# Decay rows by a DRAM round trip: eight broadcast loads in place of 24 matmuls in a chunked scan

## The chip, the cores and the metric

The kernel runs on one core of a Trainium2 chip. The metric is the device time of one execution in microseconds (us); three runs of the kernel before were timed, and one execution of it was profiled.

## The reference, cut to what matters

The layer has a mixer (a state-space scan with 8 heads in 2 groups beside 8 attention heads), an output projection with a norm, and a mixture of 16 experts with a second norm, on 512 tokens of 1024 channels. The change touches one matrix of the scan. With `da = dt * a` per token and head, cumulated within a chunk, the reference has

```
a_cum = jnp.cumsum(da, axis=2)
seg = a_cum[:, :, :, None] - a_cum[:, :, None, :]
lmat = jnp.exp(jnp.where(tri, seg, -jnp.inf))
cb = jnp.einsum('bclgn,bcsgn->bclsg', cc, bc)
y_diag = jnp.einsum('bclsg,bclsgr,bcsgrp->bclgrp', cb, lmat, xdt)
```

So for each chunk and head a matrix exp(a_cum[l] - a_cum[s]) is needed for s <= l, and zero above; it is multiplied by C B^T. The kernel takes chunks of 128 tokens (4 of them) where the reference takes 64; the result is the same sum.

## The kernel before, in words

One core does everything in two phases. The first has the input projection, the scan, the attention and the output projection (until about 303 us of the span), with the router after it; the second has the experts, whose weights stream in from DRAM. All tiles of 4 KB a partition come from one pool of 31 slabs (`U`, L163), handed out in the order of the program text, each as an earlier one is released.

TensorE (PE) runs in the order of the program text. Work is written as generators that yield TensorE microseconds, and `weave` (L866) lets the fill stream (projections of group 1, values, queries and keys) run for as long as the chain asks. For VectorE (DVE), ScalarE (ACT), GpSimd (POOL) and SyncE's DMA queue (SP) no order is written down here: the framework's planner places their instructions by its own model of the time, and each engine then runs its queue in that order. The DMA queue of SP waits in place: an issue that waits for its buffer holds those behind it. Its loads around the scan are the projection weights `wr` (L224), 512 KB each, three buffers.

`gates` (L355) makes the decays. `pcum` (L396) are sums of `da` over the tokens of a chunk by a matmul with a triangle of ones (`triones`, L316); `acum` (L398) is [token, (chunk, head)] with the totals beside it. L414 transposes it to 64 rows (chunk, head), ACT and DVE split these into two exact parts `acT` (L416), and POOL spreads them over a group's four heads with a mask, `RL` (L420, four instructions of 64x512). The masks come from POOL instructions at the start (`hmask` L317 to L320, `cself` L322 to L326) and a cast by DVE (`csel` L327).

`scan` (L532) runs once a group, `decay` (L542) once a chunk and group, eight times in all. TensorE puts row l of the cumulated decays on all partitions with two matmuls 128x512 (L547: `csel` picks the chunk's rows of `RL`) and adds the causal mask with a third (L548), all into the PSUM bank `pl`. Three more make C B^T in `pcb` (L551). Then DVE subtracts the column of `acum` (L553, one instruction 128x512, from PSUM), ACT takes the exponential (L555), DVE multiplies by `pcb` (L556), and ACT and DVE split the product into `mt` (L557, through L103 and L104). `mt` is read by the matmuls of `py` (L586, L588). The decays of chunks 0 and 1 stand ahead of the loop (L567, L569), the one of chunk c+2 in the middle of chunk c (L602).

Beside these, `conv2` (L434) runs four DVE instructions for each block of 128 channels: three taps (L437), a correction of three columns (L438), and the gate (L440) behind ACT's tanh (L439). `conv_in` (L428) empties the PSUM bank of a projection (L429, ACT). POOL splits weights: `wl` (L234, 128x512, four a unit).

Of the kernel before, what the change touches and what calls it, by code (L numbers as in the profile page):

```python
# [7 lines left out]
F32 = mybir.dt.float32  # L8
F32R = mybir.dt.float32r
# [7 lines left out]
P = 128  # L17
S = 512
D = 1024
NT = S // P  # L20
# [52 lines left out]
# whose down projections follow an expert's gate and up projections  # L73
DOWN = [[]] + [[e - 1] for e in range(1, NEXP - 3)] + [[NEXP - 4, NEXP - 3], [NEXP - 2], [NEXP - 1]]
# order of the steps of the last norms: of a tile's, or the last expert's
# [7 lines left out]
def hybrid_layer(ctx: ExitStack, tc: tile.TileContext, x, xT, wu, w16, bT, bz, bv, b16, cw, cb,  # L83
# [22 lines left out]
    # ---- constants that depend on shapes alone  # L106
# [10 lines left out]
    # strict[j, l] = 1 where j < l  # L117
# [10 lines left out]
    # -big above the diagonal (column > row), and below it  # L128
# [11 lines left out]
    def rsqrt(o, var, mult, add, eng=V):  # L140
        """o = (var * mult + add) ** -0.5 on [P, n]"""
        eng.tensor_scalar(o, var, mult, add, op0=OP.mult, op1=OP.add)
        G.tensor_tensor(o, o, mhalf[:, : o.shape[1]], op=OP.pow)
# [5 lines left out]
    # tokens' places with each expert (1 and up, 0 for none), and what an expert's list holds  # L149
    # of a token: its number (less BIG) in two parts and its weight in three, exact in bfloat16  # L150
# [8 lines left out]
    # slabs of 4 KB and of 1 KB a partition, shared by all phases  # L159
# [17 lines left out]
    # ---- x^T and the columns of w_in as exact pairs of float32r parts  # L177
# [7 lines left out]
    def first_x(q, n):  # L185
        """x^T of two blocks of channels, in n parts: first the loads, then the splits"""
# [14 lines left out]
    def first_w(u, q, n):  # L201
        """half of a unit's columns, likewise"""
# [38 lines left out]
    # The tensor engine runs in the order of emission. Work is written as generators that  # L241
    # yield the tensor engine's microseconds, so that independent streams can be woven.
    def proj_T(u, m, r):
        """r gets out[channel, token] of 128 channels of a unit"""
        pt = bank("pj", "pjT")
        i = 0
        for k in range(KC):
            h_, l_ = units[u][k // 4]
            for w_, x_ in ((h_, xh), (h_, xl), (l_, xh)):
                T.matmul(pt, lhsT=w_[:, k % 4, m * P:(m + 1) * P], rhs=x_[k], start=(i == 0), stop=(i == 23))  # L250
                i += 1
            yield 0.64
        r.append(pt)

    def proj_T2(u, r):
        """both halves of a unit together, block by block as these arrive"""
# [10 lines left out]
    def proj_R(u, t, r):  # L267
        """r gets out[token, 256 channels] for one tile of tokens"""
# [10 lines left out]
    # ---- the first loads, in the order of their use  # L279
# [9 lines left out]
    # ---- per-channel parameters  # L289
# [17 lines left out]
    # rows (chunk, head) of a 64-row table: which head, which chunk  # L307
    hmask = const.tile([64, 8], F32, name="hmask")
    triones, csel = halves("csel")
    csel = csel[:64].rearrange("p (c l) -> p c l", l=P)  # L310
    # triones[j, l] = 1 where j <= l
    trionesf, cself = halves("cself", F32)
# [4 lines left out]
    G.memset(hmask, 0.0)  # L317
    for c in range(NT):
        G.affine_select(out=hmask, in_=hmask, compare_op=OP.not_equal, fill=1.0, base=-8 * c,
                        pattern=[[-1, 8]], channel_multiplier=1)  # L320
    cself = cself[:64].rearrange("p (c l) -> p c l", l=P)
    G.memset(cself, 1.0)  # L322
    G.affine_select(out=cself, in_=cself, compare_op=OP.is_ge, fill=0.0, base=0,
                    pattern=[[-8, NT], [0, P]], channel_multiplier=1)
    G.affine_select(out=cself, in_=cself, compare_op=OP.is_ge, fill=0.0, base=7,
                    pattern=[[8, NT], [0, P]], channel_multiplier=-1)  # L326
    V.tensor_copy(csel, cself)  # L327
    # bias of the convolution's input: what all four taps add, and what the first
    # three tokens lack of it
# [16 lines left out]
    # ---- dt and the forget gates: [token, tile, (dt 8 | f 8)]  # L346
# [6 lines left out]
    RL = {}  # L353

    def gates():  # L355
# [15 lines left out]
        # softplus(v) = max(v, 0) + log1p(exp(-|v|)); log1p(e) = 2 atanh(e / (2 + e))  # L371
# [13 lines left out]
        # decays: da = dt * a, a = -exp(a_log)  # L385
        V.scalar_tensor_tensor(da, sp[:, :, 0:8], -1.0, an[:, None, :].to_broadcast([P, NT, 8]), op0=OP.mult, op1=OP.mult)
        V.tensor_scalar(dth, sp[:, :, 0:8], 0.5, None, op0=OP.mult)
        # 8 log f of head h on 16 copies each
# [5 lines left out]
        # cumulative sums within 128-token chunks, and their totals  # L394
# [8 lines left out]
        # rows -8 F[s]: partition (a, h) holds head h  # L403
# [8 lines left out]
        # the chunks' cumulative sums as rows (chunk, head), spread over a group's heads  # L412
        pa = bank("t", "pa")
        T.transpose(pa[:64, :P], acum, identf)  # L414
        ath, atl = (t_[:64] for t_ in halves("acT"))
        split(ath[:, :P], atl[:, :P], pa[:64, :P])  # L416
        for g in range(2):
            RL[g] = halves(f"RL{g}")
            for o_, a_ in zip(RL[g], (ath, atl)):
                G.tensor_tensor(o_[:64].rearrange("p (h l) -> p h l", l=P),  # L420
                                a_[:, None, :P].bitcast(F32).to_broadcast([64, 4, P]),
                                hmask[:, 4 * g:4 * g + 4, None].to_broadcast([64, 4, P]), op=OP.mult)
# [3 lines left out]
    # ---- state-space heads, one group of four heads at a time  # L426
# [6 lines left out]
    def conv2(in_, blk):  # L433
        """2 silu(conv(proj + bias)) of 128 channels: [channel, token]"""  # L434
# [12 lines left out]
    def tt4(o, a, sc4, op, eng=V):  # L447
        """o[p, 256] = a[p, 256] op sc4[p, head]"""
# [8 lines left out]
    def prep(g):  # L457
        """projections, convolution and operands of a group's scan"""
# [37 lines left out]
        # hi and lo parts side by side, so that one pass serves both  # L496
# [35 lines left out]
    def scan(g):  # L532
        """yields the time that the tensor engine may be given to other work"""
# [8 lines left out]
        def decay(c):  # L542
            # decay matrix times C B^T: [s, (head, l)]
            cs = slice(c * P, (c + 1) * P)
            pl = bank("s", "pl")
            for i in range(2):
                T.matmul(pl, lhsT=csel[:, c], rhs=RL[g][i][:64], start=(i == 0), stop=False)  # L547
            T.matmul(pl, lhsT=identb, rhs=maskl[:, None, :].to_broadcast([P, 4, P]), start=False, stop=True)  # L548
            pcb = bank("t", "pcb")[:, :P]
            for i, (b_, c_) in enumerate((("bh", "ch"), ("bh", "cl"), ("bl", "ch"))):  # L550
                T.matmul(pcb, lhsT=w[b_][:, cs], rhs=w[c_][:, cs], start=(i == 0), stop=(i == 2))  # L551
            lt = U("lt")[:, :512].rearrange("p (h l) -> p h l", l=P)
            V.tensor_tensor(lt, pl.rearrange("p (h l) -> p h l", l=P),  # L553
                            ac3[:, c, hs][:, :, None].to_broadcast([P, 4, P]), op=OP.subtract)
# [16 lines left out]
        for c in range(NT):  # L571
# [37 lines left out]
            # 2 silu(z) y, normed over the group's channels  # L609
# [18 lines left out]
    # ---- attention  # L628
    # (a head's hi and lo parts of v lie side by side, and those of its q one over the other,
    # so that one pass serves both)  # L630
# [56 lines left out]
    def head_S(hd, t):  # L687
# [9 lines left out]
        # -logits, and minus their maximum  # L697
# [42 lines left out]
    def heads():  # L740
        """yields the time that the tensor engine may be given to other work"""
# [42 lines left out]
    # ---- output projection; the state-space half of it fills the end of the attention  # L784
# [32 lines left out]
    # ---- router on rows u before their norm: logits = rs (u g wr - mu 1 g wr) + (b wr + br)  # L817
# [19 lines left out]
    # ---- weaving  # L837
# [54 lines left out]
    # ---- expert weights stream in from here on  # L892
    raw = {}

    def pieces():
        """the experts' weights in the order of their use: (expert, piece)"""
# [32 lines left out]
    # ---- experts  # L929
# [605 lines left out]
```

## Time and profile before

| what | us |
|---|---|
| median of three runs | 652.01 |
| lowest, highest | 650.62, 652.3 |
| span of the profiled execution (first to last instruction) | 649.7 |
| TensorE busy in the span | 586.1 |
| VectorE busy | 529.2 |
| ScalarE busy | 415.5 |
| GpSimd busy | 248.7 |

The own time of the profiled execution is not among the three runs that are given: its span stands 2.3 us under their median, and that difference is taken as what lies around the span. In the profile every row has a start or a count, a busy time, the engine, the line (L553 is line 553) and the tiles (out<-in). What stands behind an arrow in brackets is the idle time before the row and what ended it. A busy TensorE is back to back, not at its peak.

### The profile page before, as it was taken

The page shows a single profiled execution, that of the slowest core. Times are in us where ns is not written, and L with a number is a line of the kernel's source. Part 1 is how long each engine was busy: PE and PEld are TensorE (multiplying, and loading weights), DVE is VectorE, ACT ScalarE, POOL GpSimd, SP SyncE. Part 2 cuts the span into 40 slices and gives each one's busy share as a digit, 9 for nine tenths or more (in the row PEclk, how much of TensorE's full clock was granted, in tenths as well). Part 3 has the DMA queues.
Part 4 walks back from the last instruction along what each step waited for, and adds up shares of the span by engine and source line. Part 5 has one row for each costly group of instructions (what it writes and reads, how often), then busy time and mean ns, then how long its engine had stood idle before and what let it go on. Part 6 is the DMA issues. An engine that isn't in the chain of part 4 may idle for free.

```text
span 649.7 us, 9097 instructions
## 1 busy us (share of the span) xinstructions
PE 586.1 (90%) x3007; PEld 477.0 (73%) x3007; DVE 529.2 (81%) x869; ACT 415.5 (64%) x629; POOL 248.7 (38%) x248
## 2 busy tenths in 40 slices
PE   5888996999999999999398999999999999999950
PEld 4677786888776767788277888888888888877830
DVE  3986789688658797765879999999999999999673
ACT  5443353443577875523267888888888888887770
POOL 6537623733452341015614223333333322310282
PEclk9897997999999999998589999999999999999985
DMA  8421122211111174994888999999999999992342
GB/s 263 137 74 54 65 66 66 82 66 64 66 66 45 47 238 134 369 370 165 307 293 307 320 371 358 382 361 352 346 350 341 366 343 361 322 361 55 115 176 83
DMA packets 61702, 141.39 MB, mean 218 GB/s; under 512 B 9987, under 2 KB 10003, under 8 KB 61648
## 3 DMA queue, kind: packets, MB, share of 16 engines
q1 hardware_dynamic: 55168, 125.79, 54.1%
q0 software_dynamic: 5904, 12.85, 7.1%
q10 hardware_dynamic: 576, 2.10, 0.8%
q8 instruction: 25, 0.41, 0.3%
q14 instruction: 29, 0.24, 0.1%
HBM read 134.69 MB, written 14.68 MB: 230 GB/s over the span
## 4 chain that ended last, share of the span: by engine, by line
PE 62%; DVE 13%; ACT 6%; issue 6%; DMA 6%; POOL 5%; SPq 0%; POOLq 0%; ACTq 0%; DVEq 0%
PE pw L809 6%; PE pg L1003 5%; PE pg L1005 4%; PE pg L1004 4%; PE py L1037 4%; PE pu L1003 4%; PE pu L1005 4%; PE pu L1004 4%; PE py L1039 4%; PE py L1038 4%; PE pjT L250 4%; PE pjR L274 3%; DVE acc L437 3%; PE pxg L979 2%; DMA wr<-in_wu 1%
## 5 line engine op out<-in xcount | busy, mean ns | idle before, releaser
L986 ACT ACTIVATE eh<-wf 128x1024 fp32r<-128x1024 f32 x192 | 203.1, 1061 | 49.8 <-PE pg L1005 15.2
L234 POOL TENSOR_TENSOR wl<-wr,wh 128x512 fp32r<-128x512 f32 x40 | 57.0, 1449 | 45.0 <-ACT wh L229 42.2
L957 POOL DMA_INDIRECT xg<-hb,ix x16 | 21.1, 1317 | 112.7 <-PE pg L1005 107.5
L1043 POOL DMA_INDIRECT ub<-yo,ix x15 | 27.2, 1811 | 88.7 <-ACT at L103 54.4
L1037 PE MATMUL py<-eh,at 128*128 128x512 f32 x128 | 52.5, 410 | 2.7 <-ACT at L103 2.5
L1003 PE MATMUL pg<-eh,xgh 128*128 128x512 f32 x128 | 53.1, 415 | 0.8 <-ACT xgh L103 0.8
L1039 PE MATMUL py<-eh,at 128*128 128x512 f32 x128 | 50.9, 398 | 0.0
L1005 PE MATMUL pg<-eh,xgl 128*128 128x512 f32 x128 | 50.7, 396 | 0.0
L1003 PE MATMUL pu<-eh,xgh 128*128 128x512 f32 x128 | 50.0, 391 | 0.0
L1005 PE MATMUL pu<-eh,xgl 128*128 128x512 f32 x128 | 49.9, 390 | 0.0
L250 PE MATMUL pjT<-xh,wh 128*128 128x512 f32 x112 | 46.3, 413 | 1.6 <-DVE kl L672 1.6
L274 PE MATMUL pjR<-wh,xh 128*128 128x256 f32 x128 | 39.3, 307 | 8.6 <-ACT acc L429 7.6
L250 PE MATMUL pjT<-xh,wl 128*128 128x512 f32 x112 | 44.1, 394 | 0.0
L250 PE MATMUL pjT<-xl,wh 128*128 128x512 f32 x112 | 43.9, 392 | 0.0
L936 POOL TENSOR_SCALAR se<-seats,place 128x128 bf16<-128x128 f32 x56 | 43.5, 792 | 0.5
L274 PE MATMUL pjR<-wl,xh 128*128 128x256 f32 x128 | 38.1, 298 | 0.0
L274 PE MATMUL pjR<-wh,xl 128*128 128x256 f32 x128 | 38.0, 297 | 0.0
L274 PEld LDWEIGHTS pjR<-wh,xh 128*128 128x128 f32 x128 | 26.3, 206 | 9.3 <-ACT acc L429 8.0
L1037 PEld LDWEIGHTS py<-eh,at 128*128 128x128 f32 x128 | 24.5, 191 | 8.6 <-ACT at L103 2.7
L1005 PEld LDWEIGHTS pg<-eh,xgl 128*128 128x128 f32 x128 | 24.3, 190 | 6.1 <-DVE xgl L104 0.8
L1039 PEld LDWEIGHTS py<-eh,at 128*128 128x128 f32 x128 | 24.4, 191 | 5.9 <-DVE at L104 0.8
L1003 PEld LDWEIGHTS pg<-eh,xgh 128*128 128x128 f32 x128 | 24.3, 190 | 5.0 <-ACT xgh L103 1.2
(951 smaller groups left out, 1757.7 us busy)
## 6 DMA issues: line engine op xcount, KB each, us to landing
wf<-in_w_up SPq DMA_DIRECT2D x64, 512.0 KB
wf<-in_w_gate SPq DMA_DIRECT2D x64, 512.0 KB
wf<-in_w_down SPq DMA_DIRECT2D x60, 512.0 KB
wr<-in_wu SPq DMA_DIRECT2D x22, 512.0 KB
wor<-in_w_out SPq DMA_DIRECT2D x8, 512.0 KB
hh<-in_x SPq DMA_DIRECT2D x4, 512.0 KB
wf<-in_w_down POOLq DMA_DIRECT2D x4, 512.0 KB, 7.9
u<-ub SPq DMA_DIRECT2D x4, 512.0 KB
```

The costliest lines, as they stand in the source:

```text
L234: G.tensor_tensor(l_[:, j], wr_[:, j], h_[:, j].bitcast(F32), op=OP.subtract)
L250: T.matmul(pt, lhsT=w_[:, k % 4, m * P:(m + 1) * P], rhs=x_[k], start=(i == 0), stop=(i == 23))
L274: T.matmul(pt, lhsT=x_[k][:, t * P:(t + 1) * P], rhs=w_[:, k % 4, :], start=(i == 0), stop=(i == 23))
L809: T.matmul(pw, lhsT=m_[k][:, ts_], rhs=wo[k][w_][:, c_], start=(i == 0), stop=(i == 11))
L936: eng.tensor_scalar(r[t], seats, place_(t), None, op0=OP.is_equal)
L986: A.activation(h_, src, AF.Copy)
L1003: T.matmul(pt, lhsT=h_[:, k], rhs=wh_[:, f], start=(k == 0), stop=False)
L1004: T.matmul(pt, lhsT=h_[:, k], rhs=wl_[:, f], start=False, stop=False)
L1005: T.matmul(pt, lhsT=l_[:, k], rhs=wh_[:, f], start=False, stop=(k == KC - 1))
L1037: T.matmul(pt, lhsT=h_[:, f], rhs=wh_[:, c_], start=(f == 0), stop=False)
L1039: T.matmul(pt, lhsT=l_[:, f], rhs=wh_[:, c_], start=False, stop=(f == 3))
L1043: G.indirect_dma_start(out=ub, out_offset=bass.IndirectOffsetOnAxis(ap=ix, axis=0), in_=yo, in_offset=None, bounds_check=S - 1, oob_is_err ...
```

## The change

`gates` no longer makes `RL`: it transposes the 32 rows of cumulated decays, copies them to SBUF with ACT and writes them to a DRAM tile `ad` [chunk, head, token] through SP's queue. `decay` loads the four rows of its group and chunk onto all 128 partitions (`al`, 2 KB a partition) through SP's queue, and DVE subtracts the column and adds the mask, one instruction a head, in place of the single subtraction. The three matmuls of `pl` are gone, and `hmask`, `csel` and their making. The rest of the diff deletes comments.

```diff
-    hmask = const.tile([64, 8], F32, name="hmask")
-    triones, csel = halves("csel")
-    csel = csel[:64].rearrange("p (c l) -> p c l", l=P)
-    trionesf, cself = halves("cself", F32)
+    triones, trionesf = U("triones", F32R)[:, :512], U("trionesf")[:, :512]
     G.memset(trionesf, 1.0)
     G.affine_select(out=trionesf, in_=trionesf, compare_op=OP.is_ge, fill=0.0, base=0,
                     pattern=[[1, S]], channel_multiplier=-1)
     V.tensor_copy(triones, trionesf)
-    G.memset(hmask, 0.0)
-    for c in range(NT):
-        G.affine_select(out=hmask, in_=hmask, compare_op=OP.not_equal, fill=1.0, base=-8 * c,
-                        pattern=[[-1, 8]], channel_multiplier=1)
-    cself = cself[:64].rearrange("p (c l) -> p c l", l=P)
-    G.memset(cself, 1.0)
-    G.affine_select(out=cself, in_=cself, compare_op=OP.is_ge, fill=0.0, base=0,
-                    pattern=[[-8, NT], [0, P]], channel_multiplier=1)
-    G.affine_select(out=cself, in_=cself, compare_op=OP.is_ge, fill=0.0, base=7,
-                    pattern=[[8, NT], [0, P]], channel_multiplier=-1)
-    V.tensor_copy(csel, cself)
...
-    RL = {}
+    ad = tc.dram_tile([NT, 8, P], F32, name="ad")
...
         pa = bank("t", "pa")
-        T.transpose(pa[:64, :P], acum, identf)
-        ath, atl = (t_[:64] for t_ in halves("acT"))
-        split(ath[:, :P], atl[:, :P], pa[:64, :P])
-        for g in range(2):
-            RL[g] = halves(f"RL{g}")
-            for o_, a_ in zip(RL[g], (ath, atl)):
-                G.tensor_tensor(o_[:64].rearrange("p (h l) -> p h l", l=P),
-                                a_[:, None, :P].bitcast(F32).to_broadcast([64, 4, P]),
-                                hmask[:, 4 * g:4 * g + 4, None].to_broadcast([64, 4, P]), op=OP.mult)
+        T.transpose(pa[:32, :P], acum[:, 0:32], identf)
+        at_ = U("acT")[:32, :P]
+        A.activation(at_, pa[:32, :P], AF.Copy)
+        SY.dma_start(ad.rearrange("c h l -> (c h) l"), at_)
...
         def decay(c):
             cs = slice(c * P, (c + 1) * P)
-            pl = bank("s", "pl")
-            for i in range(2):
-                T.matmul(pl, lhsT=csel[:, c], rhs=RL[g][i][:64], start=(i == 0), stop=False)
-            T.matmul(pl, lhsT=identb, rhs=maskl[:, None, :].to_broadcast([P, 4, P]), start=False, stop=True)
+            al = U("al")[:, :512].rearrange("p (h l) -> p h l", l=P)
+            SY.dma_start(al, ad[c:c + 1, hs, :].to_broadcast([P, 4, P]))
...
             lt = U("lt")[:, :512].rearrange("p (h l) -> p h l", l=P)
-            V.tensor_tensor(lt, pl.rearrange("p (h l) -> p h l", l=P),
-                            ac3[:, c, hs][:, :, None].to_broadcast([P, 4, P]), op=OP.subtract)
+            for r in range(4):
+                V.scalar_tensor_tensor(lt[:, r], al[:, r], ac3[:, c, 4 * g + r:4 * g + r + 1], maskl, op0=OP.subtract, op1=OP.add)
             A.activation(lt, lt, AF.Exp)
```

## Rows read from the trace of the kernel before

**Rows 1.** Stages: length, busy PE, PEld, DVE, ACT, POOL (count), clock, DMA, GB/s.

```profile
48.00:64.00 16.00, 12.40 (x79) 12.03 (x80) 10.95 (x19) 6.14 (x14) 12.01 (x13) 0.79 0.20 66
64.00:80.00 16.00, 16.00 (x78) 12.01 (x77) 11.50 (x19) 7.25 (x13) 9.96 (x10) 1.00 0.20 66
80.00:96.00 16.00, 15.61 (x85) 12.77 (x84) 14.19 (x28) 8.20 (x16) 4.36 (x5) 1.00 0.20 67
96.00:112.00 16.00, 10.89 (x62) 10.47 (x61) 14.99 (x27) 7.85 (x15) 6.91 (x6) 0.79 0.21 67
...
128.00:144.00 16.00, 15.69 (x123) 14.43 (x121) 12.66 (x27) 8.15 (x19) 6.27 (x5) 1.00 0.24 81
144.00:160.00 16.00, 15.25 (x104) 13.88 (x105) 14.02 (x32) 6.22 (x16) 5.87 (x5) 1.00 0.11 34
...
400.00:432.00 32.00, 32.00 (x158) 26.28 (x157) 30.64 (x39) 26.74 (x32) 10.99 (x12) 1.00 1.00 358
```

**Rows 2.** The chain that ended last, 56 to 65 us: start, length, work.

```profile
56.41 4.36 PE pjR L274 x24
...
60.98 2.86 PE pjR L274 x24
...
64.28 0.66 PE pl L547 x2
64.94 0.32 PE pl L548
```

**Rows 3.** Timeline of VectorE at the start: start, busy, line, out<-in.

```profile
17.49 1.65 DVE L231 TENSOR_TENSOR wl<-wr,wh 128x1024 fp32r<-128x1024 f32 x1
19.06 0.41 DVE L327 CAST csel<-cself 64x512 fp32r<-64x512 f32 x1
19.39 1.21 DVE L231 TENSOR_TENSOR wl<-wr,wh 128x1024 fp32r<-128x1024 f32 x1
```

**Rows 4.** Timelines of GpSimd and of VectorE, 49 to 56 us.

```profile
49.84 5.63 POOL L420 TENSOR_TENSOR RL<-acT,hmask 64x512 fp32r<-64x512 f32 x4
...
49.66 2.22 DVE L437 SCALAR_TENSOR_TENSOR acc<-acc,cw_sb 128x511 f32<-128x511 f32 x2
...
52.13 1.19 DVE L437 SCALAR_TENSOR_TENSOR acc<-acc,cw_sb 128x509 f32<-128x509 f32 x1
53.24 0.99 DVE L438 TENSOR_TENSOR acc<-acc,lack 128x3 f32<-128x3 f32 x1
...
54.99 1.03 DVE L440 SCALAR_TENSOR_TENSOR acc<-acc 128x512 f32<-128x512 f32 x1 [0.42 <-ACT acc L439]
```

**Rows 5.** The same instructions of VectorE while GpSimd stands idle, 90 to 92 us.

```profile
90.93 0.74 DVE L437 SCALAR_TENSOR_TENSOR acc<-acc,cw_sb 128x509 f32<-128x509 f32 x1
91.59 0.16 DVE L438 TENSOR_TENSOR acc<-acc,lack 128x3 f32<-128x3 f32 x1
```

**Rows 6.** VectorE's subtractions for `lt` and `v`, by tile: min/median/max ns, starts.

```profile
L553 DVE TENSOR_TENSOR lt<-pl,acum x8: 675/684/692, 67.2 to 149.8; 128x512 f32<-128x512 f32 x8
...
L104 DVE TENSOR_TENSOR v<-vf,v x16: 281/284/1378, 128.5 to 156.8; 128x128 fp32r<-128x128 f32 x16
```

**Rows 7.** Groups of VectorE, 40 to 176 us, shapes apart: busy us, mean ns.

```profile
L104 DVE TENSOR_TENSOR v<-vf,v 128x128 fp32r<-128x128 f32 x16 | 7.2, 489 | 0.4 <-ACT v L103 0.4
```

**Rows 8.** A decay's subtraction, and the idle time of GpSimd around it.

```profile
93.45 0.68 DVE L553 TENSOR_TENSOR lt<-pl,acum 128x512 f32<-128x512 f32 x1
...
95.94 0.67 POOL L143 TENSOR_TENSOR rst<-rst,mhalf 128x1 f32<-128x1 f32 x1 [8.49 <-DVE rst L142]
```

**Rows 9.** ACT's copy of the rows, SP's next issue behind it, and one 256 KB broadcast load.

```profile
48.66 0.26 ACT L103 ACTIVATE acT<-pa 64x128 fp32r<-64x128 f32 x1
...
66.35 0.33 SPq L224 DMA_DIRECT2D wr<-in_wu  x1
...
L635 SPq DMA_DIRECT2D bv_sb<-in_bv x1: 376/376/376, 123.0 to 123.0; - x1
...
L646 DVE TENSOR_TENSOR vf<-pjR,bv_sb x8: 411/418/425, 127.3 to 154.0; 128x256 f32<-128x256 f32 x8
```

## The prediction

> **What bounds the kernel now.** The page's first part comes first: TensorE is busy for most of the span, VectorE next. An average over stages says nothing of one place, so the table of stages follows, then the chain that ended last, and the timelines of VectorE, GpSimd and SP. In the table of stages [rows 1] the reader is to see two regimes. TensorE is full at 64 to 80 us (16.00 of 16), and nearly so at 80 to 96, 128 to 144 and 144 to 160. Between, at 96 to 112, it has 10.89 of 16 while VectorE has 14.99: there VectorE is the bound, and TensorE waits for it. VectorE has little room at 80 to 96 (14.19) and at 144 to 160 (14.02) either. From 400 us on TensorE is full (32.00 of 32), so time won before is kept, one for one, unless the weights' loads fall behind; those start when the first phase gives its slabs free, so they move with it.
>
> In the chain [rows 2] the decays' matmuls stand on the path: 0.66 us for the two of L547 and 0.32 for the mask of L548, 0.98 us a decay, behind pjR matmuls of the fill stream. The chain's stretch before them goes over VectorE's conv instructions at 49 to 56 us, and these are long there only because GpSimd makes `RL` at the same time: three taps and the correction take 2.22, 1.19 and 0.99 us [rows 4], where at 90 us, with GpSimd idle, the same forms take 0.74 and 0.16 [rows 5].
>
> **The start.** GpSimd makes fewer masks and VectorE loses the cast of `csel`, 0.41 us. The subtraction of `wl` beside the masks took 1.65 us, the next one 1.21 [rows 3]. If the first also gets 1.21, VectorE is 0.44 + 0.41 = 0.85 us earlier where the convolution starts. I take -0.85; the bound on the other side is 0, if a load is late next.
>
> **RL goes.** Four GpSimd instructions, 5.63 us [rows 4]. A free pair of taps costs one step and one duration, 91.59 - 90.93 = 0.66, and 0.74, together 1.40 us [rows 5]. So the pair gives back 2.22 - 1.40 = 0.82, the third tap 1.19 - 0.74 = 0.45, the correction 0.99 - 0.16 = 0.83: 2.10 us, all ahead of the gate of L440, for which TensorE's next transposes wait. Between 0 and 2.10 I take 2.10, since nothing else of GpSimd's stands in those 6 us. The gate is left at its 1.03 us. The split of `acT` on VectorE goes too; it hid in a wait for ACT and counts nothing.
>
> **TensorE's clock.** At 48 to 64 us the granted clock was 0.79 [rows 1], behind idle TensorE, and 24 pjR matmuls took 4.36 us, the next 24 2.86 [rows 2]. With 2.10 us less idle ahead the first may come nearer to the second: between 0 and 1.50 us. I take 0.5, nearer to none, because part of that idle time stays.
>
> **The eight decays' matmuls.** 8 x 0.98 = 7.84 us of TensorE go. Where TensorE is full they count: those of chunks 0 and 1 of group 0, at 64 to 80 us, give 1.96 us. Chunks 2 and 3 come just ahead of the stretch where TensorE waits for VectorE; I count nothing for them (bound 1.96). Of group 1, whose last subtraction starts at 149.8 [rows 6], in nearly full stages [rows 1], I count three of four, 2.94 us (bounds 1.96 and 3.92).
>
> **VectorE's four instructions for one.** The subtraction takes 684 ns at the median [rows 6]. No 128x128 instruction with a pointer scalar is in the trace; the nearest is the 128x128 subtraction of `v` from SBUF, 284 ns at the median [rows 6]. Behind one another such instructions step by 0.08 us less than they last (0.74 against 0.66 [rows 5]), so four make 0.284 + 3 x 0.204 = 0.90 us, 0.22 more a decay, 1.8 in all. On the path I count the three decays where VectorE is short: +0.6 (bounds 0 and 1.8). [...]
>
> **GpSimd and VectorE together.** L553 reads PSUM and one SBUF tile and never stretched: 675 to 692 ns over eight [rows 6]. The new instructions read `al` and the mask, both in SBUF, like the taps, which did stretch. Lower bound: nothing, since seven of the eight subtractions stood where GpSimd was idle, as at 93.45 within an idle time of 8.49 us [rows 8]. Upper: the 16 subtractions of `v` of 128x128 took 489 ns on average against 281 at the least [rows 6, 7], 0.21 more, times 32 is 6.7 us. I take one decay's worth on the path, 4 x 0.21 = +0.8, nearer to the idle places.
>
> **The new loads.** ACT's copy, now one in place of a split, ends at 48.92; the write of 16 KB and then a broadcast load follow on SP's queue. The nearest row is a 256 KB broadcast load issued at 123.0 whose first reader ran at 127.3 [rows 9], so at most 4.3 us. Two in a row end before 48.9 + 8.6 = 57.5, and the first use was at 67.2. SP issues nothing before 66.35 [rows 9]; its wait for the write holds nobody. The other loads need a slab, and with `RL` and the masks gone three long-held slabs are free. DMA share is 0.20 there [rows 1]; 2 MB more are no load. I cost all this at nothing. ACT gains nothing; its exponential is the same.
>
> **Sum.** -0.85 - 2.10 - 0.5 - 1.96 - 2.94 + 0.6 + 0.8 = -6.95 us. The profiled span is 649.7, so 642.75; the median stands 2.3 us above that span, which gives 645.0 us. That is 1.1% faster. Its own range, with the bounds above mixed, is about 641 to 649.
>
> **Rivals.** *VectorE hides it.* Where TensorE waits for VectorE in any case, TensorE's savings turn into longer waits: the 4.9 us of matmuls and the 0.5 of clock fall away, and -0.85 - 2.10 + 0.6 + 0.8 = -1.55 remains: 650.5. For it: VectorE's 14.99 and 14.02 of 16. Against it: 16.00 of 16 for TensorE at 64 to 80. Chance 0.17.
>
> *Slower: the two engines lock each other.* If the mask additions fall into GpSimd's bursts of weight splits, each waits for a GpSimd instruction, as the correction of L438 did for 0.83 us: 4 x 0.83 = 3.3 us a decay. Five decays stand where VectorE is short (two of group 0, three of group 1): 16.6 us, less the 8.35 saved, plus 0.6, is +8.9, or 660.9; with four of them hit 657.5. It decides from 7.75 us on the path, between two and three decays. Against it speaks that seven of eight places are free now; for it that the planner may move them. [...] Chance 0.12.
>
> *The rows come late.* If the planner puts the first load behind the blocked weight load, it is issued at 66.7 and lands at 71.0, 3.8 us behind the old subtraction. Then what was saved before it is lost in a wait of TensorE, and +3.8 - 0.98 - 2.94 + 1.4 = +1.3 gives 653.3. It would mean also that the change does not do what it says, since a DMA's wait then stands in place of the matmuls. Chance 0.07.
>
> **Numbers.** A measurement of this kernel tells about 0.3%, 2 us, from no change. Forecast 0.64, hidden 0.17, locked 0.12, late 0.07. The range 640.5 to 653.5 goes from the forecast with more of the clock and of the matmuls up to the late rows, and leaves out most of the locked case and the forecast's far ends, about 0.18. Faster: the forecast and a third of the hidden case, 0.70. Same: the rest of the hidden case and most of the late one, 0.17. Slower: 0.13.
>
> **What would show it.** Right: no matmul of `pl`; the taps at 49 us at 0.74; mask additions of about 0.28 us each; every `al` landed well before its first reader; TensorE's transposes near 56 us some 3 us earlier, and the attention 7 us earlier. Wrong: mask additions of 0.5 us and more on average, an idle VectorE that a load ends, or a TensorE whose idle time at 96 to 112 us grows by what the matmuls gave back.

## The result and the profile after

The changed kernel takes **662.3 us** (median), the kernel before 652.2 us in the same comparison: a ratio of 1.0164, with a 95% interval of 1.0139 to 1.0189. The forecast was 645.0 us and faster; the kernel is slower by 1.6% and lies outside the range. The profiled execution's span went from 649.7 to 660.0 us. TensorE is busy 581.1 us in it (586.1 before), VectorE 530.2 (529.2), GpSimd 240.5 (248.7).

The table of stages of the changed kernel, with the columns of [rows 1]:

```profile
48.00:64.00 16.00, 12.69 (x94) 11.81 (x95) 11.44 (x23) 7.51 (x16) 10.22 (x12) 1.00 0.22 75
64.00:80.00 16.00, 14.95 (x79) 12.54 (x77) 10.71 (x21) 7.04 (x13) 7.68 (x8) 1.00 0.29 92
80.00:96.00 16.00, 9.06 (x36) 6.98 (x36) 12.77 (x25) 4.83 (x10) 3.58 (x4) 0.79 0.28 82
96.00:112.00 16.00, 7.33 (x40) 6.45 (x39) 11.16 (x21) 8.13 (x14) 6.29 (x5) 0.78 0.27 82
```

At 48 to 64 us the start is as forecast: the granted clock is 1.00 where it was 0.79. At 64 to 80 us TensorE has lost 1.05 us (14.95 for 16.00). At 80 to 112 us it has 16.39 us of work where it had 26.50 [rows 1], and VectorE is less busy as well (23.93 for 29.18): both wait. Most of the loss is made there. It is read from the output transposes `pms`, whose first and last starts are, now and before:

```profile
L541 PE MATMUL pms<-identf,zs x16: 270/272/421, 115.0 to 189.6; 128*128 128x128 f32 x16
```

```profile
L563 PE MATMUL pms<-identf,zs x16: 270/272/421, 106.0 to 178.3; 128*128 128x128 f32 x16
```

Group 0 is 9.0 us later, group 1 adds 2.3 us, and after that the distance nearly stays: the experts' first transposes (`pxg`) come at 325.6 us before and 336.2 now.

VectorE's timeline of the changed kernel, first the taps of [rows 4], then the mask additions of the four decays of group 0:

```profile
49.48 1.59 DVE L417 SCALAR_TENSOR_TENSOR acc<-acc,cw_sb 128x511 f32<-128x511 f32 x2 [0.29 <-ACT acc L410]
...
51.33 0.74 DVE L417 SCALAR_TENSOR_TENSOR acc<-acc,cw_sb 128x509 f32<-128x509 f32 x1
51.99 0.16 DVE L418 TENSOR_TENSOR acc<-acc,lack 128x3 f32<-128x3 f32 x1
...
66.93 1.72 DVE L532 SCALAR_TENSOR_TENSOR lt<-al,acum,maskl 128x128 f32<-128x128 f32 x4 [3.60 <-DMA al<-ad]
...
87.86 1.13 DVE L532 SCALAR_TENSOR_TENSOR lt<-al,acum,maskl 128x128 f32<-128x128 f32 x4
...
104.92 1.14 DVE L532 SCALAR_TENSOR_TENSOR lt<-al,acum,maskl 128x128 f32<-128x128 f32 x4 [1.90 <-DMA al<-ad]
```

The taps run free, as forecast. The additions for chunks 2 and 3 start at 87.86 and 104.92, where the old subtractions started at 82.75, shown here from the kernel before, and at 93.45 [rows 8]:

```profile
82.75 0.68 DVE L553 TENSOR_TENSOR lt<-pl,acum 128x512 f32<-128x512 f32 x1
```

Why is on SP's queue, whose timeline of the changed kernel shows each row load of group 0 right behind a weight load:

```profile
50.15 0.42 SPq L402 DMA_DIRECT2D ad<-acT  x1
62.40 0.33 SPq L224 DMA_DIRECT2D wr<-in_wu  x1
62.78 0.42 SPq L526 DMA_DIRECT2D al<-ad  x1
65.66 0.33 SPq L224 DMA_DIRECT2D wr<-in_wu  x1
66.03 0.43 SPq L526 DMA_DIRECT2D al<-ad  x1
79.27 4.00 SPq L224 DMA_DIRECT2D wr<-in_wu  x2
83.36 0.38 SPq L526 DMA_DIRECT2D al<-ad  x1
99.95 0.33 SPq L224 DMA_DIRECT2D wr<-in_wu  x1
100.38 0.39 SPq L526 DMA_DIRECT2D al<-ad  x1
```

It is the weight loads that wait, for their buffer. The list of the queue's own waits, 40 to 160 us (in all, times, longest), has these two rows and none of a load of `al`, so neither the rows' slab nor their write held one:

```profile
SPq L224 <- ACT wh L229: 84.6, 9, 21.0
SPq L224 <- POOL wl L234: 33.8, 12, 3.4
```

The row loads' time from issue to landing (min/median/max), in the changed kernel:

```profile
DMA to landing us min/median/max: 3.8/4.1/4.3
```

The write is issued at 50.15 us, but the first load only at 62.78; it lands some 4.1 us later, when VectorE has been idle for 3.60 us. Chunk 2's load, issued at 83.36, would by that median land near 87.5, and its addition follows at 87.86, behind other work of VectorE. The list of VectorE's and TensorE's waits, 40 to 192 us of the changed kernel (in all, times, longest):

```profile
DVE lt L532 <- DMA al<-ad: 7.1, 3, 3.6
...
PE pjR L274 <- ACT acc L409: 9.6, 2, 8.7
PE pbt L469 <- DVE lt L534: 6.8, 1, 6.8
```

TensorE's `pbt` waits 6.8 us: its PSUM bank is held by `pcb` until VectorE has multiplied the late chunk 2 (89.70 us). The longest wait, 8.7 us up to 109.07, has chunk 3 behind it. There TensorE waits for ScalarE to empty a bank (L409), and ScalarE's timeline shows that this stands in its queue behind the exponential and the split of the late chunk 3:

```profile
106.09 0.63 ACT L533 ACTIVATE lt<-lt 128x512 f32<-128x512 f32 x1 [2.47 <-DVE lt L532]
107.90 0.63 ACT L103 ACTIVATE mt<-lt 128x512 fp32r<-128x512 f32 x1 [1.18 <-DVE lt L534]
108.43 0.58 ACT L409 ACTIVATE acc<-pjT 128x512 f32<-128x512 f32 x1
```

Behind the first idle time the projection's matmuls of 512 columns step by 0.43 us for some 3 us, in place of 0.23; behind the second those of 256 columns step by 0.21 us for some 6 us, in place of 0.12. So a late load is paid several times: as VectorE's wait, as TensorE's, and in the clock that follows TensorE's idle time. The granted clock is 0.79 and 0.78 in the two stages; before it was 1.00 and 0.79, so the clock's loss is new in the first one only.

### The profile page after: what moved, and what is told of

It is laid out like the page before. It is cut to its first block, busy times and chain, and to the rows that moved or that the text cites. A ratio compares the mean times of both kernels' runs of the same rounds, so it can differ in the third digit from the quotient of the medians.

```text
span 660.0 us, 9078 instructions
## 1 busy us (share of the span) xinstructions
PE 581.1 (88%) x2983; PEld 475.2 (72%) x2983; DVE 530.2 (80%) x891; ACT 415.7 (63%) x629; POOL 240.5 (36%) x236
## 5 line engine op out<-in xcount | busy, mean ns | idle before, releaser
L250 PE MATMUL pjT<-xh,wh 128*128 128x512 f32 x112 | 48.8, 436 | 3.3 <-DVE kl L650 3.0
L250 PE MATMUL pjT<-xh,wl 128*128 128x512 f32 x112 | 46.2, 413 | 0.0
L250 PE MATMUL pjT<-xl,wh 128*128 128x512 f32 x112 | 45.8, 409 | 0.0
L250 PEld LDWEIGHTS pjT<-xh,wh 128*128 128x128 f32 x112 | 22.6, 202 | 8.0 <-issue 3.4
## 6 DMA issues: line engine op xcount, KB each, us to landing
wf<-in_w_down SPq DMA_DIRECT2D x60, 512.0 KB, 11.8
```

## The experiments

Times are medians, with the 95% interval of the ratio to the kernel before in brackets; the kernel before had medians of 652.0 to 652.3 us beside them. One ratio is known to about 0.2%, so a difference of two kernels to some 1.7 us.

### When the rows arrive

**All loads behind the write.** The eight loads are issued in `gates`, into four slabs.

```diff
         SY.dma_start(ad.rearrange("c h l -> (c h) l"), at_)
+        for g in range(2):
+            for c in range(NT):
+                if c % 2 == 0:
+                    a2 = U("al")
+                AL[g, c] = a2[:, (c % 2) * 512:(c % 2 + 1) * 512].rearrange("p (h l) -> p h l", l=P)
+                SY.dma_start(AL[g, c], ad[c:c + 1, 4 * g:4 * g + 4, :].to_broadcast([P, 4, P]))
...
-            al = U("al")[:, :512].rearrange("p (h l) -> p h l", l=P)
-            SY.dma_start(al, ad[c:c + 1, hs, :].to_broadcast([P, 4, P]))
+            al = AL[g, c]
```

> All eight row loads are issued right behind the write of the rows, ahead of the blocked weight loads. Late rows (the loads stood on SP's queue behind weight loads that wait for their buffer): the four waits of VectorE for a load go, the first subtraction starts near 64 to 65 us in place of 66.9, that of group 0's last chunk near 92 in place of 104.9, TensorE's idle time at 96 to 112 us is no larger than the 5.1 us of before, and the time is 644 to 650. Rival, VectorE's four instructions for one and their contention cost the time: all rows are early and the time stays at 655 or above, with VectorE as full as in the changed kernel. Rival, VectorE hides TensorE's saving: 650 to 652.

650.5 us [0.9961 to 0.9996]: 11.8 us under the changed kernel, and faster than before by 0.2%. The loads are issued from 53.5 to 56.8 us (the first 3.7 us behind the write), no addition waits for one, chunk 3's addition starts at 92.30 in place of 104.92, and `pms` at 100.5 in place of 115.0. That is the late rows' branch, just above its 650. The mask additions in this kernel, the loads, and `pms`:

```profile
L538 DVE SCALAR_TENSOR_TENSOR lt<-al,acum,maskl x32: 339/346/1409, 62.2 to 144.0; 128x128 f32<-128x128 f32 x32
L409 SPq DMA_DIRECT2D al<-ad x8: 326/430/472, 53.5 to 56.8; - x8
```

```profile
L547 PE MATMUL pms<-identf,zs x16: 271/272/273, 100.5 to 176.2; 128*128 128x128 f32 x16
```

**Another queue.** The changed kernel with the loads issued from ScalarE's queue, at the same place of the text.

```diff
-            SY.dma_start(al, ad[c:c + 1, hs, :].to_broadcast([P, 4, P]))
+            A.dma_start(al, ad[c:c + 1, hs, :].to_broadcast([P, 4, P]))
```

> The changed kernel with each row load issued from ScalarE's queue in place of SP's, where no weight load stands ahead of it. Late rows: no subtraction waits over 1 us for a load except perhaps the first, the idle time of 8.7 us of TensorE near 100 us goes, and the time is 646 to 654; what is left depends on how far ahead the planner puts each issue among ScalarE's work. Rival, VectorE's instructions: 658 or more as in the changed kernel.

661.75 us (one run): a miss, nothing is won. No weight load stands ahead of the loads now, yet they are issued at 60.28, 68.22, 84.97 and 99.36 us for group 0, and VectorE waits for six of the eight, 7.7 us in all. ScalarE's timeline shows the third behind instructions that waited for VectorE:

```profile
83.58 0.63 ACT L419 ACTIVATE acc<-acc 128x512 f32<-128x512 f32 x1 [5.59 <-DVE acc L418]
84.96 0.63 ACT L424 ACTIVATE b<-acc 128x512 fp32r<-128x512 f32 x1 [0.76 <-DVE acc L420]
84.97 0.33 ACTq L526 DMA_DIRECT2D al<-ad  x1
```

So the theory that the weight loads alone are the cause falls. What is common to both queues is that a load stands where the text has it, just ahead of its decay, and whatever waits there holds it. The next run tests that.

**Two decays ahead.** The loads stay on SP's queue between the weight loads, but each is written two decays earlier.

```diff
+    def load_rows(g, c):
+        AL[g, c] = U("al")[:, :512].rearrange("p (h l) -> p h l", l=P)
+        SY.dma_start(AL[g, c], ad[c:c + 1, 4 * g:4 * g + 4, :].to_broadcast([P, 4, P]))
...
+        for c in range(2):
+            load_rows(0, c)
...
+            al = AL[g, c]
+            if (g, c) < (1, 2):
+                load_rows(g + (c + 2) // 4, (c + 2) % 4)
```

> The changed kernel with each load put two decays earlier in the program text, still on SP's queue between the same weight loads. If what makes the loads late is their place in the text, just ahead of their use: near the run with all loads early, 650 to 652.5, with no wait of VectorE for a load over 0.5 us. If any place behind a blocked weight load is too late: 654 or more, with waits for loads of group 0's chunks 2 and 3.

651.0 us [0.9962 to 1.0]: the first branch. SP's timeline has the third and fourth load at 62.56 and 65.92 us, almost the slots that the first two have in the changed kernel, each again behind a weight load; but they are now two decays ahead of their use, and no addition waits for one:

```profile
53.43 0.80 SPq L344 DMA_DIRECT2D al<-ad  x2
62.18 0.33 SPq L224 DMA_DIRECT2D wr<-in_wu  x1
62.56 0.42 SPq L344 DMA_DIRECT2D al<-ad  x1
```

From the same queue, written two decays earlier, the loads cost 11.3 us less than in the changed kernel.

**Which loads.** First only chunks 0 and 1 of group 0 are loaded behind the write, then all four of group 0; the others stay in place. Against the first diff, the first run changes both lines and the second the upper one:

```diff
-        for g in range(2):
-            for c in range(NT):
+        for g in range(1):
+            for c in range(2):
```

> The changed kernel with only the loads of group 0's chunks 0 and 1 issued behind the write; the other six stay where they were. If the whole loss is the first two waits and what they push back: 650 to 653. If each late load costs by itself (chunks 2 and 3 of group 0, then group 1): 655 to 660, with VectorE's subtraction of chunk 3 still at 100 us or later and TensorE waiting for it.

> The changed kernel with the four loads of group 0 issued behind the write and the four of group 1 left in place. If the waits of group 0 are the whole loss: 650 to 651.5, as with all eight early. If group 1's late loads still cost what the run with two early loads lost behind its first output transposes (2.7 us): 652.5 to 654.

655.2 us [1.0027 to 1.0058] and 654.2 us [1.0018 to 1.006], the second just above its branch. The times fall where each load costs by itself, but in the first run chunk 3's addition starts at 95.72 us and not behind 100. So the first two loads are worth 7.1 us of the 11.8, chunks 2 and 3 about 1, which is within the uncertainty, and group 1 about 3.7. In the second run VectorE waits for one of group 1's loads, the first:

```profile
127.78 1.14 DVE L541 SCALAR_TENSOR_TENSOR lt<-al,acum,maskl 128x128 f32<-128x128 f32 x4 [1.07 <-DMA al<-ad]
```

The rest of the 3.7 is no wait for a row load; TensorE's waits for the values' addition are longer (4.6 us for 3.4 with all loads early). That part is argued from the difference of two runs, and is the least certain.

### What VectorE's four instructions cost

**The mask on VectorE in the kernel before.** The rows come from TensorE as before, its mask matmul is dropped, and VectorE adds the mask in four instructions from PSUM.

```diff
-            T.matmul(pl, lhsT=identb, rhs=maskl[:, None, :].to_broadcast([P, 4, P]), start=False, stop=True)
...
-            V.tensor_tensor(lt, pl.rearrange("p (h l) -> p h l", l=P),
-                            ac3[:, c, hs][:, :, None].to_broadcast([P, 4, P]), op=OP.subtract)
+            for r in range(4):
+                V.scalar_tensor_tensor(lt[:, r], pl[:, r * P:(r + 1) * P], ac3[:, c, 4 * g + r:4 * g + r + 1], maskl, op0=OP.subtract, op1=OP.add)
```

> The kernel before, but VectorE adds the mask in four instructions a decay from PSUM, and TensorE's mask matmul is dropped; no rows by DRAM. Late rows: VectorE pays 8 x 0.45 = 3.6 us at most and TensorE wins 8 x 0.32 = 2.6 us at most, so 650 to 655. Rival, VectorE's four instructions cost the time: most of the 10 us is here already, 658 or more.

654.7 us [1.0014 to 1.0046], as expected of the late rows: VectorE's part alone is no 10 us. But it is a loss of 2.6 us although eight matmuls are gone. The additions by tile, and two of them within a weight split of GpSimd:

```profile
L553 DVE SCALAR_TENSOR_TENSOR lt<-pl,acum,maskl x32: 334/340/346, 68.1 to 152.3; 128x128 f32<-128x128 f32 x32
```

```profile
84.55 3.06 POOL L234 TENSOR_TENSOR wl<-wr,wh 128x512 fp32r<-128x512 f32 x2 [0.91 <-ACT wh L229]
```

```profile
84.67 0.60 DVE L553 SCALAR_TENSOR_TENSOR lt<-pl,acum,maskl 128x128 f32<-128x128 f32 x2
```

Read from PSUM, none of the 32 lasts over 346 ns, beside GpSimd or not; read from SBUF, the longest lasts 1.38 us in the changed kernel and 1.41 with all loads early. So the loss here comes without any stretch of the additions.

**Twice the additions.** The kernel with loads two decays ahead, with the four additions of each decay made into an unread tile first.

```diff
+            l2 = U("l2")[:, :512].rearrange("p (h l) -> p h l", l=P)
+            for o_ in (l2, lt):
+                for r in range(4):
+                    V.scalar_tensor_tensor(o_[:, r], al[:, r], ac3[:, c, 4 * g + r:4 * g + r + 1], maskl, op0=OP.subtract, op1=OP.add)
```

> The kernel with loads two decays ahead (651.0 us), with each decay's four mask additions made twice, the first time into an unread tile: 8 x 1.05 = 8.4 us more of VectorE. By the forecast's rule that three decays of eight count: 3 x 1.05 = 3.2 us, 654 to 655. If every us of VectorE there counts: 8.4 us, 659 to 660, and with the stretching of the first decay's instructions doubled too 661 to 663.

657.6 us [1.0077 to 1.0113], between the two branches. VectorE's groups in that kernel (busy us, mean ns), the doubled instructions first:

```profile
L542 DVE SCALAR_TENSOR_TENSOR l<-al,acum,maskl 128x128 f32<-128x128 f32 x32 | 15.7, 531 | 0.0
L542 DVE SCALAR_TENSOR_TENSOR lt<-al,acum,maskl 128x128 f32<-128x128 f32 x32 | 10.0, 372 | 0.0
```

and the one group in the kernel with loads two decays ahead:

```profile
L540 DVE SCALAR_TENSOR_TENSOR lt<-al,acum,maskl 128x128 f32<-128x128 f32 x32 | 14.8, 511 | 0.0
```

25.7 - 14.8 = 10.9 us more of busy VectorE cost 657.6 - 651.0 = 6.6 us, 0.6 a us. The old subtractions were 8 x 0.684 = 5.5 us [rows 6], so four for one with its stretched instructions is 9.3 us more, and at 0.6 some 5.6 us of time. That is an estimate from these rows, and a rough one: over the whole span VectorE is only 8.7 us busier (538.6 for 529.9), which makes 0.75 a us and some 7 us.

**One SBUF operand.** The four instructions subtract and take the minimum with 0; C B^T is masked once instead, `maskl` being a triangle of ones here.

```diff
-                V.scalar_tensor_tensor(lt[:, r], al[:, r], ac3[:, c, 4 * g + r:4 * g + r + 1], maskl, op0=OP.subtract, op1=OP.add)
+                V.tensor_scalar(lt[:, r], al[:, r], ac3[:, c, 4 * g + r:4 * g + r + 1], 0.0, op0=OP.subtract, op1=OP.min)
...
+            pcm = Q("pcm")[:, :P]
+            V.tensor_tensor(pcm, pcb, maskl, op=OP.mult)
+            V.tensor_tensor(lt, lt, pcm[:, None, :].to_broadcast([P, 4, P]), op=OP.mult)
```

> The kernel with loads two decays ahead, where VectorE's four instructions subtract the column and take the minimum with 0 (one SBUF operand instead of two), C B^T is masked once by a triangle of ones, and the product stays one instruction; VectorE has as many instructions and one of 128x128 more. If contention with GpSimd of the mask additions' two SBUF operands costs: none of the four lasts over 0.4 us, the first decay takes 1.0 to 1.2 us in place of 3.4, and the time is 1.5 to 4 us lower, 647 to 649.5. If only their number and length cost: 650.5 to 652.

657.9 us [1.0064 to 1.0131], a miss on both branches. The instructions by tile, and the wait of TensorE that ends at 144.56 us in its timeline:

```profile
L540 DVE TENSOR_SCALAR lt<-al,acum x32: 274/281/1351, 62.9 to 147.3; 128x128 f32<-128x128 f32 x32
```

```profile
144.56 0.39 PE L274 MATMUL pjR<-wh,xh 128*128 128x256 f32 x1 [3.28 <-DVE rst L142]
```

One SBUF operand did not free them: up to 1.351 us still, and the product, now with two SBUF operands, up to 1.155 us. The first decay's four take 3.18 us, where 1.0 to 1.2 was expected. `tensor_scalar`, at 281 ns in the median, runs no faster than the 284 of the subtraction of `v` [rows 6], and is held up as well. That one SBUF operand would be enough was the author's estimate; the nearest row, L553 with 692 ns at most [rows 6], has its other operand in PSUM. So the run does not tell contention from number. What makes it slower comes after `pms`, which starts earlier here (101.7 us) than with the loads two decays ahead (104.3): in group 1 TensorE waits 3.28 us, and the granted clock is 0.60 at 144 to 150 us. Why VectorE's order differs there stays open.

### What the removed work was worth

**Matmuls put back.** The kernel with all loads early, and three matmuls into an unread bank in each decay.

```diff
+            pl = bank("s", "pl")
+            for i in range(3):
+                T.matmul(pl, lhsT=w["bh"][:, cs], rhs=w["ch"], start=(i == 0), stop=(i == 2))
             pcb = bank("t", "pcb")[:, :P]
```

> The kernel with all loads early (650.5 us), with three matmuls of 128x512 into an unread bank put back ahead of C B^T in each decay, so TensorE does about the work that the change removed. If VectorE hides what TensorE saved (rival VectorE hides it): 650 to 652, at most 1.5 us over the run with early loads, and TensorE's idle time at 100 to 126 us smaller. If TensorE's saving counted as the forecast had it: 4.9 us over it, 654.5 to 656.

654.2 us [1.0005 to 1.0043], 3.7 us more (3.0 by the ratios), just under the second branch and nearer to the forecast's 4.9 than to nothing. Which decays count is not told cleanly. `pms` of group 0 starts at 99.4 us with them and at 100.5 without, so those of group 0 do not show there; the last `pcb` stands at 152.5 against 147.3. But 1.7 of these 5.2 us stand already at 110.76, ahead of group 1's first decay, where TensorE waits 4.99 us for VectorE's `acc` (3.42 without them).

**RL put back.** The kernel with all loads early, and four GpSimd instructions into unread tiles. The first run has them behind ScalarE's copy, reading it on 32 partitions; the second, shown here, ahead of it.

```diff
+        for g in range(2):
+            for o_ in halves(f"RL{g}"):
+                G.tensor_tensor(o_[:64].rearrange("p (h l) -> p h l", l=P), identf[:64, None, :].to_broadcast([64, 4, P]),
+                                acum[:64, 4 * g:4 * g + 4, None].to_broadcast([64, 4, P]), op=OP.mult)
```

> The kernel with all loads early, with four GpSimd instructions of 32x512 put back behind ScalarE's copy, as RL's were, into unread tiles. If RL's removal is kept to the end: 2.1 us over the run with early loads, 652 to 653.5; the taps near 49 to 53 us take 2.2 and 1.2 us again. If what is won at 56 us is lost to VectorE at 96 to 112 us: within 0.7 us of it, 650 to 651.2.

656.6 us [1.0047 to 1.0086], a miss on both branches and not a price of RL: the planner put the four at 55.02 us, ahead of weight splits that then met VectorE. One 128x256 instruction, 0.42 us in the kernel before at 111.06 us, with GpSimd idle, lasts 7.99 here:

```profile
59.73 7.99 DVE L515 SCALAR_TENSOR_TENSOR zs<-zth,zf 128x256 f32<-128x256 f32 x1 [1.96 <-ACT zth L514]
```

> The kernel with all loads early, with four GpSimd instructions of 64x512 put back, reading the cumulated decays and an identity, so that they can run where RL's did (49 to 56 us). The forecast's term: the taps near 49 to 53 us take 2.2 and 1.2 us again, and the end is 2.1 us later than with early loads alone, 652 to 653.5. If what they cost there is lost to VectorE's later bound anyway: 650 to 651.2.

654.0 us [1.0021 to 1.0049], 3.5 us more, above both branches. Here they stand where RL stood, and VectorE's timeline has the taps and the correction of [rows 4] back to within 0.01 us (the pair of taps too, 2.23):

```profile
51.69 1.19 DVE L428 SCALAR_TENSOR_TENSOR acc<-acc,cw_sb 128x509 f32<-128x509 f32 x1
52.80 0.99 DVE L429 TENSOR_TENSOR acc<-acc,lack 128x3 f32<-128x3 f32 x1
```

### A kernel that beats both

**ScalarE subtracts.** With early loads, ScalarE takes the column within the exponential; VectorE masks C B^T once by a triangle of ones and caps at 1, since above the diagonal the exponential may be large.

```diff
+        V.tensor_scalar(nac, acum[:, 0:32], -1.0, None, op0=OP.mult)
...
-            for r in range(4):
-                V.scalar_tensor_tensor(lt[:, r], al[:, r], ac3[:, c, 4 * g + r:4 * g + r + 1], maskl, op0=OP.subtract, op1=OP.add)
-            A.activation(lt, lt, AF.Exp)
-            V.tensor_tensor(lt, lt, pcb[:, None, :].to_broadcast([P, 4, P]), op=OP.mult)
+            for r in range(4):
+                A.activation(lt[:, r], al[:, r], AF.Exp, bias=nac[:, 8 * c + 4 * g + r:8 * c + 4 * g + r + 1])
+            pcm = Q("pcm")[:, :P]
+            V.tensor_tensor(pcm, pcb, maskl, op=OP.mult)
+            V.scalar_tensor_tensor(lt, lt, 1.0, pcm[:, None, :].to_broadcast([P, 4, P]), op0=OP.min, op1=OP.mult)
```

> The early loads, and the column is subtracted by ScalarE within the exponential (four instructions of 128x128 with the negative column as bias), while VectorE multiplies C B^T once by a 0/1 triangle and then takes the minimum with 1 and the product in one instruction of 128x512; VectorE has 1.0 us a decay in place of 1.8, ScalarE has four instructions for one. Late rows with VectorE's share second: 1 to 3 us under the run with early loads alone, 642 to 648. If ScalarE is the short one there, equal to that run or above it.

> As the run before, with ScalarE's subtraction within the exponential and C B^T masked once. If both parts add: 648 to 650, 1.8 us under the run before, and 2 to 4 us under the kernel before the change. If ScalarE, with four instructions for one, now waits for loads: 650 or more.

With all loads early 648.7 us [0.9934 to 0.9974], 1.8 under the run without it and just above its range; with loads two decays ahead 647.6 us [0.992 to 0.9956], 3.4 under, which is more than expected.

**The bias of the values.** With timely rows the next late load is one that the change never touched: in the kernel with loads two decays ahead `bv_sb` is issued on SP's queue at 121.25 us, VectorE waits 5.5 us for it and TensorE 4.3 us for VectorE's addition of it (1.1 in the kernel before). The first try put it behind the eight early loads, the next two behind the fourth row load.

```diff
+            if (g, c) == (0, 1):
+                AL["bv"] = U("bv_sb")[:, :512]
+                SY.dma_start(AL["bv"], bcast_rows(bv, 512))
...
-        bv_sb = U("bv_sb")[:, :512]
-        SY.dma_start(bv_sb, bcast_rows(bv, 512))
+        bv_sb = AL["bv"]
```

> The kernel with early loads and ScalarE's subtraction (648.7 us), with the load of the values' bias issued behind the row loads too, in place of behind the weight loads at 121 us. TensorE's waits for the values' addition (2.8 us in the run before this) go: 646 to 648. If those waits only hide VectorE's next one: 648 to 649.5.

> The kernel with row loads two decays ahead (651.0 us), with the load of the values' bias put behind the fourth row load in the program text, near 66 us in place of 121 us. If the values' wait for it holds the missing time: VectorE's addition no longer waits for that load, TensorE's waits for it fall from 4.3 us to about 1, and the time is 647 to 649.5. If VectorE's next work takes its place: 650 to 652.

> The same on the kernel with ScalarE's subtraction (647.6 us). If the wait for the bias holds time: 644.5 to 646.5. If not: 647 to 649.

The first gives 649.9 us [0.9939 to 0.9983], 1.2 over the run without it and a miss on both branches. In its profiled execution, the slowest of six with 652.5 us, the first decay's product starts at 71.75 us against 67.47, far ahead of the place where the load is read, so it does not judge the load; why that decay is late stays open. The second gives 649.6 us [0.9946 to 0.9991], 1.4 under the run without it and just above its expectation, with 2.5 us of TensorE's wait left where about 1 was expected; the third **645.35 us [0.9847 to 0.9948]**, 2.3 under its own, as expected of a wait that holds time, and about 1.0% under the kernel before. The load in the third, whose first reader starts at 119.6 us, then TensorE's wait from 108 to 192 us:

```profile
L539 SPq DMA_DIRECT2D bv_sb<-in_bv x1: 430/430/430, 66.7 to 66.7; - x1
```

```profile
PE pjR L274 <- DVE vf L637: 1.7, 2, 1.1
```

Neither gain, 1.4 or 2.3 us, is clear of the uncertainty by itself (the third run's interval alone is some 6.6 us wide); that both point the same way speaks for the load.

## Why the prediction was wrong

The time is 17.3 us above the forecast's 645.0. Rows in time take 11.8 of them away (650.5); the other 5.5 are not the rows' lateness.

**The new loads** are the step that failed: "I cost all this at nothing". It measured 11.3 and 11.8 us. The step reckoned the loads' earliest time (two end before 57.5 us) and took it for their time. It noted that SP issues nothing before 66.35 us, but read that as a free queue; it is a queue held by a weight load, and a load written just ahead of its decay gets its place behind it (issued at 62.78 us behind the weight load of 62.40). Its other fear, the slab, was rightly put aside: no load of `al` waited for one.

**The rival of the late rows** had the mechanism: issued at 66.7, landing at 71.0. Measured were 62.78 and an addition at 66.93, so earlier. But it priced the first load alone, 653.3 us, at a chance of 0.07. The later loads are late in the same way (83.36 and 100.38 us, each right behind a weight load), and the wait moves VectorE's whole order, holds a PSUM bank of TensorE's (6.8 us), and is followed by a lower clock (0.79 for 1.00 at 80 to 96 us).

**VectorE's four instructions** were the second step to fail: +0.6 for the length and +0.8 for the contention, where the estimate from the doubling gives 5.6 or more. An addition lasts 346 ns in the median and not 284, and four make 1.13 us and not 0.90. With early rows the first decay's four take 4.63 us, since they fall into GpSimd's weight splits (from 62.14 and 65.31 us); yet that one stretch is hidden. The product behind it starts at 67.49 us, and where ScalarE subtracts, with all loads early too, at 67.47, because there VectorE waits 4.42 us for ScalarE's exponential.

**RL** was put at 2.10 with 0.5 of clock, and 3.5 was measured; **the decays' matmuls** at 4.9, and 3.7 was measured. Both differences lie within the 1.7 us to which two kernels can be told apart, so neither term is shown to be mis-sized. **The start** gives 0.18 us at the first taps (49.66 to 49.48), not 0.85; the taps wait there for ScalarE (0.29 us).

Put together, with timely rows: -0.2 - 3.5 - 3.7 + 5.6 = -1.8, and 650.5 and 651.0 were measured, 1.7 and 1.2 under the kernel before. The terms add up within their uncertainty, which is larger than the sum. How the 5.6 splits between length and contention was not separated; the run with the mask on VectorE, where no addition is stretched (346 ns at most), shows that length and number alone cost 2.6 us and whatever its eight missing matmuls gave back. Late rows add 11.8 to this, which is no check of the sum, being the difference of the two kernels itself.

Two rivals come near by chance. The 650.5 of the one in which VectorE hides the gain is what timely rows give, but by other terms. The 660.9 of the one in which the two engines lock each other is near the 662.3, but by another cause: with early rows the additions are stretched as much (up to 1.41 us), and the time is 650.5.

**Right** were the free taps, the loads' own 4.1 us, and the sign that would tell: "an idle VectorE that a load ends", and TensorE's idle time at 96 to 112 us growing from 5.11 to 8.67.

## What to carry to other kernels

A load put in place of work has two times: how long it takes (here 4.1 us), and when its issue gets its turn (here 12.6 us behind the write). Read the second from the queue's own timeline, with what waits ahead at that place of the text, and write the load a stage or two earlier than its reader (two decays were worth 11.3 us here); another queue doesn't help if its engine waits as well (661.75 us from ScalarE's). When a load goes late in a pipeline, price the second wait (who holds which bank, what stands behind it in the other engines' queues, what the clock does behind the idle time, here 0.79 for 1.00), not the first alone.

## What the runs showed of the hardware

VectorE's 128x128 instruction with a column as scalar and two SBUF operands takes 346 ns in the median (335 at the least), and up to 1.42 us beside GpSimd; from PSUM its 32 took 334 to 346. The `tensor_scalar` with one SBUF tensor takes 281 ns in the median and was stretched to 1.351 us too. ScalarE's exponential of 128x128 with a column as bias takes 387 ns, and four of them overlap to 1.26 us against 0.63 for one of 128x512. The broadcast loads of the rows, 256 KB each, took 3.8 to 4.3 us from issue to landing in the changed kernel and, with loads two decays ahead, 3.7 to 4.1, or 3.4 to 4.4 where ScalarE subtracts. With all loads early, and two decays ahead with and without ScalarE's subtraction, the first of them follows the 16 KB write that it reads directly, and was issued 3.5 to 3.7 us behind that write.
